# Mixer projections split at 400 and 240 tokens, first feed-forward loaded in three groups

## The chip, the cores and the metric

The kernel runs on one core of a Trainium2 chip. Its time is the device time of one launch in microseconds (us); three runs of the kernel before gave 3033.8, 3035.15 and 3030.21 us, median 3033.8. TensorE (PE in the rows) multiplies matrices, VectorE (DVE), ScalarE (ACT) and GpSimd (POOL) work on tiles, and SyncE (SP) issues the DMAs.

## The reference

One decoder layer over 1040 tokens (16 learned meta tokens and 1024 of the input), 1024 channels, in float32:

```
h = concat([meta, x])
h = h + 0.5 * swiglu(rms_norm(h, ffn1_norm), ffn1_w_in, ffn1_w_out)
h = h + hybrid_mixer(rms_norm(h, mix_norm), w_in, ...)     # DeltaNet branch | retention branch
h = h + 0.5 * swiglu(rms_norm(h, ffn2_norm), ffn2_w_in, ffn2_w_out)
out = rms_norm(h, final_norm)[:, 16:]
```

The mixer projects the normed tokens with one matrix of 1024 rows into queries, keys, values and gates of both branches (8 heads of 128 columns each), and two times 1024 columns for the merging gates. In the retention branch queries and keys are turned by a rotary table before the scan over chunks.

## The kernel before

Channels lie on the partitions and tokens along the free dimension. Each float32 operand is split into a high and a low part in the fp32r type, and `mm3` (L155 to L160) issues three matmuls for one product: high by high, high by low, low by high. A split (`split`, L135) is a copy on ScalarE and a subtraction on GpSimd, or on VectorE where the caller asks for it (`eng=V`).

The program runs through these stages: loading, transposing and norming the tokens for the first feed-forward (`start_group`, `start_operands`); the first feed-forward; `tail1`, which adds its last part and makes the mixer's operands; the retention heads (`ret_proj`, `ret_scan`); the gates and the DeltaNet heads, woven together; the output products; the second feed-forward.

A mixer projection takes a pair of output columns (128 each) at a time. Its scheme saves products: the tokens are cut into two halves of `HM` and a rest of `RM`, and the 1024 channels into two halves of four 128-row pieces. For the two token halves seven products (with sums of weights and sums of operands) replace eight; each is 4 pieces x 3 matmuls = 12 matmuls of HM columns, 84 a pair. The rest is computed plainly (`plain`): 16 pieces x 3 = 48 matmuls of RM columns a pair. With HM = 344, RM is 352. There are 40 such pairs: 16 for retention, 16 for DeltaNet, 8 for the gates. Beside them, the same token blocks (`MIX3`) cut the last part of the first feed-forward (48 matmuls a block) and the small products of `ab_products` (24, 24 and 36 split over the blocks: 60 of HM columns, 24 of RM).

For the first two retention heads the plain part and two of the products come ahead (`project_plain`, four pairs), since they need only the operands of the rest and of the first half; the operands of the five other products are made meanwhile on VectorE, ScalarE and GpSimd from the last block of the first feed-forward. Then `project_rest` does the five products; there `eng` is V, so its five weight splits a pair run on VectorE.

The order on each engine is not the order of the text: a scheduler places the instructions, and `tc.issue_after` keeps one behind another. Each engine works off its own list in order. `rotary` (L862) multiplies by a table on VectorE and GpSimd; L649 is the addition that brings a product out of PSUM.

Of the kernel before, what the change touches and what calls it, by code (L numbers as in the profile page):

```python
# [16 lines left out]
P = 128  # L17
# [29 lines left out]
    return [(a, b - a) for a, b in zip(edges, edges[1:])]  # L47


HM = 344  # L50
RM = T - 2 * HM
MIX3 = _cut([0, HM, 2 * HM, T])
REAL3 = _cut([NM, HM, 2 * HM, T])
# [43 lines left out]
def hybrid_layer(ctx, tc, a):  # L97
# [86 lines left out]
    def norm_stats(hT, b0, bn, sqs, last=None):  # L184
        for q in range(4):
            h = hT[:, 2 * q:2 * q + 2, b0:b0 + bn]
            if q == 3 and last:
                last.tensor_tensor(out=sqs[q], in0=h, in1=h, op=ALU.mult)
            else:
                S.activation(sqs[q], h, AF.Square)  # L190
        for q in range(1, 4):
            V.tensor_tensor(out=sqs[0], in0=sqs[0], in1=sqs[q], op=ALU.add)
        w = span_of(bn)
        ns = bn // w
        ps = psum("rx")
# [10 lines left out]
    def slots_of(ts, hn, n):  # L206
        return [[t[:, 4 * hn * i:4 * hn * i + 4 * hn].rearrange("p (k n) -> p k n", k=4) for t in ts] for i in range(n)]
# [67 lines left out]
    def ffn(fp, hidp, hT, hn, slots, spare, second, w_in, w_out, last_blocks, last_weights, tail, first, w0=None):  # L275
# [202 lines left out]
        for b0, bn in last_blocks:  # L478
# [5 lines left out]
                V.scalar_tensor_tensor(out=hs, in0=ps, scalar=0.5, in1=hs, op0=ALU.mult, op1=ALU.add)  # L484
            tail(b0, bn)


    f_ctx = ExitStack()
    fp = f_ctx.enter_context(tc.tile_pool(name="ffn1", bufs=4, side="right"))
# [46 lines left out]
        V.tensor_scalar(st1[:, 2, ts], st1[:, 2, ts], EPS, None, op0=ALU.add)  # L536
        rsqrt(st1[:, 3, ts], st1[:, 2, ts])

    def start_operands(grp):
        if grp == 0:  # L540
            halves = operand_halves(hidp, HN1)
            ts = [xp.tile([P, 16 * HN1], F32R, name="ox", tag="x" + t, bufs=1) for t in "HL"]
            slots[0].update(zip((0, 1, 4, 6), slots_of(ts, HN1, 4)))
        else:
            ts = [pool.tile([P, 3, 4, HN1], F32, name="b" + t, tag="e" + t, bufs=1) for pool, t in ((hidp, "H"), (fp, "L"))]
            halves = [ts[0][:, 0], ts[0][:, 1], ts[0][:, 2], ts[1][:, 0]]
            spare.extend(npool.tile([P, KC * T], F32R, name="on", tag=n) for n in ("nH", "nL"))
            slots[1].update(enumerate(slots_of(spare, HN1, 7)))
        for e in range(2):
            b0 = (2 * grp + e) * HN1  # L550
            pc = []
            for t in range(-1, NCH):
                c0, rows = (0, NM) if t < 0 else (NM + t * P, P)
                lo, hi = max(c0, b0), min(c0 + rows, b0 + HN1)
                if lo < hi:
                    pc.append((lo - b0, hi - lo, rows, lo - c0, st1[:, 3, t + 1:t + 2]))
            normed_half(hT, V_F1, b0, HN1, pc, *halves[2 * e:2 * e + 2])
        operand_blocks(slots[grp], halves, [E1[grp][i] and V or G for i in range(4)])
        return halves

    def start_differences():
# [6 lines left out]
        t = hidp.tile([P, 2, KC, P], F32R, name="ohl", tag="eH", bufs=1)  # L568
        return [[t[:, e, 4 * i:4 * i + 4] for e in range(2)] for i in range(2)]

    start_group(range(-1, 4))
    start_group(range(4, NCH))
    halves = [start_operands(grp) for grp in range(2)]
    h_d = tc.dram_tile([KC, P, SEQ], F32, name="h_d")
    ops, rest, kept, rows = [], [], [], []
    r_ctx = ExitStack()
# [1 line left out]
    def tail1(b0, bn):  # L578
        if not ops:
            n2 = [npool.tile([P, KC * T], F32R, name="act", tag=n) for n in ("nH", "nL")]  # L580
            x2 = [xp.tile([P, 16 * HN1], F32R, name="act", tag=n) for n in ("xH", "xL")]
            ops.extend(slots_of(n2, HM, 5) + slots_of(x2, HM, 2))
            for ts, o in ((n2, 20 * HM), (x2, 8 * HM)):
                rest.extend([t[:, o + k * RM:o + k * RM + RM] for t in ts] for k in range(4))
            kept.append(fp.tile([P, 12 * HN1], F32, name="sq", tag="eL", bufs=1))
        sq = kept[0][:, :KC * bn].rearrange("p (q k n) -> p q k n", q=4, k=2)
        ps = bcast(norm_stats(hT, b0, bn, [sq[:, q] for q in range(4)]), bn)

        def tmp():
            return fp.tile([P, 2 * HN1], F32, name="nrm", tag="tmp", bufs=5)[:, :bn]  # L590

        def put(i, k, src, eng):
            split(src, ops[i][0][:, k], ops[i][1][:, k], eng)

        def minus(out, x, y, eng):
            eng.tensor_tensor(out=out, in0=x, in1=y, op=ALU.subtract)

        if b0 == HM:
            hid_ctx.close()
            rows.append(r_ctx.enter_context(tc.tile_pool(name="rows", bufs=1, reuse_waits="tile")))  # L600
        if b0 == 2 * HM:
            for k in range(KC):
                n = tmp()
                normed(n.unsqueeze(1), hT, V_MIX, k, b0, bn, ps)
                split(n, *rest[k], V if k % 4 == 0 else G)
        elif b0 == 0:
            kept.append(ps)
            for k in range(KC):
                n = tmp()
                normed(n.unsqueeze(1), hT, V_MIX, k, b0, bn, ps)  # L610
                put(k // 4, k % 4, n, V if k % 4 == 0 else G)
        else:
            for k in range(4):
                b11, b21, b12, b22 = (kept[0][:, bn * i:bn * i + bn] if k % 2 else tmp() for i in range(4))
                for n, kk, t0, bc in ((b11, k, 0, kept[1]), (b12, k, HM, ps), (b22, k + 4, HM, ps), (b21, k + 4, 0, kept[1])):
                    normed(n.unsqueeze(1), hT, V_MIX, kk, t0, bn, bc)
                minus(b12, b12, b11, V)
                put(6, k, b22, V if k % 2 else G)
                minus(b22, b22, b12, V)
                put(2, k, b22, V)  # L620
                minus(b11, b22, b11, G)
                put(3, k, b11, G)
                put(4, k, b12, V)
                minus(b21, b21, b22, G)
                put(5, k, b21, G)
# [19 lines left out]

    H1, H2 = slice(0, HM), slice(HM, 2 * HM)

    def add(out, x, ps):
        V.tensor_tensor(out=out, in0=x, in1=ps, op=ALU.add)  # L649

    def product(w, i, ps=None, last=True, grow=False):
        first = ps is None
# [16 lines left out]
    def project_plain(raws, d0, d1, perm):  # L669
        a11, a12, a21, a22 = (put_weights(r, perm) for rs in raws for r in rs)  # L670
        yield from plain((a11, a12), d0)
        S.copy(d0[:, H2], (yield from product(a11, 0)))
        add(d0[:, H1], d0[:, H2], (yield from product(a12, 1)))
        yield from plain((a21, a22), d1)
        return a22

    def project_rest(raws, d0, d1, perm, a22=None):
        rg, ru = raws
        eng = None if a22 else V
        if a22 is None:  # L680
            a22 = put_weights(ru[1], perm, eng)
        V.tensor_tensor(out=ru[1], in0=ru[0], in1=ru[1], op=ALU.add)
        V.tensor_tensor(out=ru[0], in0=rg[0], in1=ru[0], op=ALU.subtract)
        V.tensor_tensor(out=rg[0], in0=ru[1], in1=rg[0], op=ALU.subtract)
        s2, s3 = put_weights(rg[0], perm, eng), put_weights(ru[0], perm, eng)
        V.tensor_tensor(out=rg[1], in0=rg[1], in1=rg[0], op=ALU.subtract)
        s1, s4 = put_weights(ru[1], perm, eng), put_weights(rg[1], perm, eng)
# [82 lines left out]
        return z[:, NM:]  # L770

    def cblk(n, pool):
        return pool.tile([P, 3 * P], F32, name="cb", tag="cb", bufs=2)[:, :n]

    ctab = tp.tile([P, T], F32, name="ctab")
    stab = tp.tile([P, T], F32, name="stab")
# [86 lines left out]
    def rotary(o):  # L863
        for b0, bn in MIX3:
            s = slice(b0, b0 + bn)
            sw = cblk(bn, rp)
            S.copy(sw[0:64], o[64:128, s])
            S.copy(sw[64:128], o[0:64, s])
            V.tensor_tensor(out=o[:, s], in0=o[:, s], in1=ctab[:, s], op=ALU.mult)
            G.tensor_tensor(out=sw, in0=sw, in1=stab[:, s], op=ALU.mult)  # L870
            V.tensor_tensor(out=o[:, s], in0=o[:, s], in1=sw, op=ALU.add)
        return o
# [689 lines left out]
```

## Time and profile before

| | |
|---|---|
| median of three runs | 3033.8 us |
| profiled execution, its own time | 3034.08 us |
| span from first to last instruction | 3032.3 us |
| TensorE busy | 2901.9 us (96%) |
| VectorE, ScalarE, GpSimd busy | 1824.1, 1341.1, 1644.4 us |
| mean granted TensorE clock | 0.978 of full |

A busy share says how much of the span an engine had an instruction in it; which engine sets the end is read stage by stage. TensorE's records overlap, since matmuls are pipelined: the pace is read from how many start in a stretch, not from the length of one. A row of windows gives the busy time of PE, PEld (weight load), DVE, ACT and POOL in that order, each with its count, then the clock, the share of the DMA engines and GB/s. "128x344" after an instruction is partitions by columns.

### The profile page before, as it was taken

The numbers are of one execution on the slowest core, as the hardware profiler recorded it, in microseconds if no ns is written. First come the engines' busy times: TensorE is split into PE (matmuls) and PEld (weight loads), VectorE is DVE, ScalarE is ACT, GpSimd is POOL, SyncE is SP. The second block draws the span as 40 slices with busy tenths as digits, with TensorE's granted clock in tenths as the row PEclk, the third lists the DMA queues.
The fourth block names the chain that finished last, engine by engine and source line by source line (L and its number), as shares of the span: only waits on it lengthen the run. The fifth ranks groups of instructions, "written<-read, shape, count | busy, mean of one in ns | idle before, by whom it ended". The sixth has DMA issues, their size and how long they took to land. (4 is left out here: it accounts for less than half of the span.)

```text
span 3032.3 us, 55807 instructions
## 1 busy us (share of the span) xinstructions
PE 2901.9 (96%) x21463; PEld 2751.1 (91%) x21463; DVE 1824.1 (60%) x3311; ACT 1341.1 (44%) x2801; POOL 1644.4 (54%) x1411
## 2 busy tenths in 40 slices
PE   7999999999999999988999999999999999998998
PEld 6999998999889999988999899988889999998877
DVE  8456557777775455455545555562338655557765
ACT  5333334433544655444555555563224433334432
POOL 5555556654655776543555554545426655557653
PEclk8999999999999999989999999999999999999999
DMA  3455557633311221212212222253533355457632
GB/s 104 137 172 160 166 172 255 211 93 119 85 50 43 67 69 58 73 46 63 76 53 64 64 82 63 58 181 113 179 102 111 117 172 170 161 162 252 209 115 94
DMA packets 368686, 359.23 MB, mean 118 GB/s; under 512 B 29073, under 2 KB 298642, under 8 KB 365858
## 3 DMA queue, kind: packets, MB, share of 16 engines
q1 hardware_dynamic: 368352, 355.64, 37.7%
q8 instruction: 168, 2.75, 0.4%
q14 instruction: 100, 0.82, 0.1%
q10 hardware_dynamic: 66, 0.02, 0.0%
HBM read 265.27 MB, written 90.32 MB: 117 GB/s over the span
## 5 line engine op out<-in xcount | busy, mean ns | idle before, releaser
L137 POOL TENSOR_TENSOR wl<-wraw,wh 128x512 fp32r<-128x512 f32 x798 | 1094.1, 1378 | 1008.3 <-ACT wh L136 940.0
L136 ACT CAST wh<-wraw 128x512 fp32r<-128x512 f32 x866 | 536.7, 623 | 976.2 <-issue 235.6
L1032 DVE SCALAR_TENSOR_TENSOR cb<-raw,cw,cb 128x344 f32<-128x344 f32 (+2 forms) x216 | 133.7, 652 | 25.1 <-ACT cb L1030 23.7
L223 DVE TENSOR_TENSOR wraw<-wraw 128x512 f32<-128x512 f32 x42 | 49.7, 1182 | 161.5 <-DMA wraw<-ffn_w_in 143.6
L158 PE MATMUL ps_gate_mm<-act,wh 128*128 128x344 f32 (+1 forms) x352 | 122.4, 348 | 6.0 <-DVE raw L649 3.9
L158 PE MATMUL ps_start_mm<-on,wh 128*128 128x260 f32 x392 | 111.6, 285 | 3.9 <-DVE q L295 2.3
L160 PE MATMUL ps_gate_mm<-act,wl 128*128 128x344 f32 (+1 forms) x352 | 114.2, 324 | 0.0
L159 PE MATMUL ps_gate_mm<-act,wh 128*128 128x344 f32 (+1 forms) x352 | 114.2, 324 | 0.0
L158 PE MATMUL ps_ffn_mm<-on,wh 128*128 128x256 f32 (+1 forms) x376 | 109.6, 292 | 2.0 <-ACT q L339 1.6
L159 PE MATMUL ps_start_mm<-on,wh 128*128 128x260 f32 x392 | 111.1, 283 | 0.0
L160 PE MATMUL ps_start_mm<-on,wl 128*128 128x260 f32 x392 | 110.8, 283 | 0.2 <-POOL wl L137 0.2
L160 PE MATMUL ps_ffn_mm<-on,wl 128*128 128x256 f32 (+1 forms) x376 | 109.5, 291 | 0.0
L159 PE MATMUL ps_ffn_mm<-on,wh 128*128 128x256 f32 (+1 forms) x376 | 109.2, 290 | 0.0
L158 PE MATMUL ps_start_px<-on,wh 128*128 128x260 f32 x308 | 87.5, 284 | 1.9 <-DVE sg L295 1.9
L298 DVE TENSOR_TENSOR q<-q,q 128x260 f32<-128x260 f32 (+1 forms) x84 | 69.7, 830 | 31.8 <-ACT q L339 31.8
L160 PE MATMUL ps_start_px<-on,wl 128*128 128x260 f32 x308 | 87.7, 285 | 0.0
L159 PE MATMUL ps_start_px<-on,wh 128*128 128x260 f32 x308 | 87.6, 285 | 0.0
L159 PE MATMUL ps_start_mm<-ox,wh 128*128 128x260 f32 x292 | 83.6, 286 | 3.6 <-DVE ox L137 3.6
L158 PE MATMUL ps_start_mm<-ox,wh 128*128 128x260 f32 x292 | 84.1, 289 | 1.7 <-ACT ox L136 1.2
L160 PE MATMUL ps_start_mm<-ox,wl 128*128 128x260 f32 x292 | 84.0, 288 | 0.6 <-POOL wl L137 0.6
L388 DVE TENSOR_TENSOR sums<-sums 128x512 f32<-128x512 f32 x80 | 83.8, 1068 | 0.7
L160 PE MATMUL ps_ffn_px<-on,wl 128*128 128x256 f32 (+1 forms) x284 | 83.2, 293 | 0.7 <-POOL wl L137 0.7
(1651 smaller groups left out, 10925.4 us busy)
## 6 DMA issues: line engine op xcount, KB each, us to landing
wraw<-ffn_w_in SPq DMA_DIRECT2D x176, 256.0 KB
wraw<-w_in SPq DMA_DIRECT2D x176, 256.0 KB
sums<-ffn_w_out SPq DMA_DIRECT2D x80, 256.0 KB
sums_d<-sums SPq DMA_DIRECT2D x20, 1024.0 KB
wraw<-sums_d SPq DMA_DIRECT2D x80, 256.0 KB
opnd<-opnd_d SPq DMA_DIRECT2D x35, 520.0 KB
opnd<-opnd_d SPq DMA_DIRECT2D x35, 512.0 KB
wraw<-ffn_w_out SPq DMA_DIRECT2D x68, 256.0 KB
```

Source lines behind the costliest of these rows:

```text
L136: S.copy(hi, raw)
L137: (eng or G).tensor_tensor(out=lo, in0=raw, in1=hi.bitcast(F32), op=ALU.subtract)
L158: PE.matmul(ps, lhsT=wh, rhs=xh, start=first and i == 0, stop=False, skip_group_check=grow)
L159: PE.matmul(ps, lhsT=wh, rhs=xl, start=False, stop=False, skip_group_check=grow)
L160: PE.matmul(ps, lhsT=wl, rhs=xh, start=False, stop=last and i == n - 1, skip_group_check=grow)
L223: V.tensor_tensor(out=ru[0], in0=ru[0], in1=ru[1], op=ALU.add)
L298: V.tensor_tensor(out=x[:, grp], in0=x[:, grp], in1=g[:, grp], op=ALU.mult)
L388: tc.keep_in_program_order(V.tensor_tensor(out=out, in0=x, in1=y, op=op))
L1032: conv[which] = V.scalar_tensor_tensor(out=c, in0=raw[:, s0 + k:s0 + k + n], scalar=cw[:, 24 * k + ct:24 * k + ct + 1], in1=c, op0=ALU.mul ...
```

## The change

`HM` becomes 400, so `RM` is 240. The operands no longer fit where they lay: the sums of squares get three slots in place of four, the last operand lies in four pieces in two places (`Pieces`), and the scratch tile `cb` grows. `project_rest` loses its `eng`, so its splits go to GpSimd. `rotary`'s first multiplication is placed behind the last `add` of the projection. `norm_stats` adds each square as soon as it is there. The tokens of the first feed-forward are loaded and normed in three groups: the tiles that the first quarter of the tokens needs, those of the second quarter, and the rest.

```diff
-HM = 344
+HM = 400
 RM = T - 2 * HM
...
-        for q in range(1, 4):
-            V.tensor_tensor(out=sqs[0], in0=sqs[0], in1=sqs[q], op=ALU.add)
+            if q:
+                V.tensor_tensor(out=sqs[0], in0=sqs[0], in1=sqs[q], op=ALU.add)
...
-    def start_operands(grp):
+    def start_operands(grp, tiles):
...
         for e in range(2):
+            if tiles[e]:
+                start_group(tiles[e])
             b0 = (2 * grp + e) * HN1
...
-    start_group(range(-1, 4))
-    start_group(range(4, NCH))
-    halves = [start_operands(grp) for grp in range(2)]
+    halves = [start_operands(0, (range(-1, 2), range(2, 4))), start_operands(1, (range(4, NCH), ()))]
...
-        sq = kept[0][:, :KC * bn].rearrange("p (q k n) -> p q k n", q=4, k=2)
-        ps = bcast(norm_stats(hT, b0, bn, [sq[:, q] for q in range(4)]), bn)
+        sq = kept[0][:, :6 * bn].rearrange("p (q k n) -> p q k n", q=3, k=2)
+        ps = bcast(norm_stats(hT, b0, bn, [sq[:, q] for q in (0, 1, 2, 1)]), bn)
...
     def add(out, x, ps):
-        V.tensor_tensor(out=out, in0=x, in1=ps, op=ALU.add)
+        added[0] = V.tensor_tensor(out=out, in0=x, in1=ps, op=ALU.add).ins
...
-    def project_rest(raws, d0, d1, perm, a22=None):
+    def project_rest(raws, d0, d1, perm):
         rg, ru = raws
-        eng = None if a22 else V
-        if a22 is None:
-            a22 = put_weights(ru[1], perm, eng)
+        a22 = put_weights(ru[1], perm)
...
-        s2, s3 = put_weights(rg[0], perm, eng), put_weights(ru[0], perm, eng)
+        s2, s3 = put_weights(rg[0], perm), put_weights(ru[0], perm)
...
-            V.tensor_tensor(out=o[:, s], in0=o[:, s], in1=ctab[:, s], op=ALU.mult)
+            with tc.issue_after(added[0]):
+                V.tensor_tensor(out=o[:, s], in0=o[:, s], in1=ctab[:, s], op=ALU.mult)
```

VectorE's list at the start of the program, before: `st` holds the statistics, `small` the diagonal that spreads them, `lower` and `ox` the first operands.

```order
L532 SCALAR_TENSOR_TENSOR st_102<-xnL 128x1
L519 BN_STATS xnL<-xnH 128x6 x2
L172 TENSOR_SCALAR small<-ident,st_102 16x16
L172 TENSOR_SCALAR small<-ident,st_102 128x128
L172 TENSOR_SCALAR small<-ident,st_102 128x116
L172 TENSOR_SCALAR small<-ident,st_102 128x12
L172 TENSOR_SCALAR small<-ident,st_102 128x128
L172 TENSOR_SCALAR small<-ident,st_102 128x120
L172 TENSOR_SCALAR small<-ident,st_102 128x8
L529 COPY hT<-ps_start_mm 128x4x128
L531 BN_AGGR xnL<-xnL 128x2
L181 SCALAR_TENSOR_TENSOR lower<-hT,wv,ps_start_px 128x260 x4
```

The same place now (the numbers of lines moved by some, L526 is L519 of before, L536 is L529, L539 is L532).

```order
L172 TENSOR_SCALAR small<-ident,st_102 16x16
L172 TENSOR_SCALAR small<-ident,st_102 128x128
L172 TENSOR_SCALAR small<-ident,st_102 128x116
L172 TENSOR_SCALAR small<-ident,st_102 128x12
L538 BN_AGGR xnL<-xnL 128x2
L536 COPY hT<-ps_start_mm 128x4x128
L539 SCALAR_TENSOR_TENSOR st_102<-xnL 128x1
L536 COPY hT<-ps_start_gx 128x4x128
L526 BN_STATS xnL<-xnH 128x6 x2
L542 TENSOR_TENSOR st_102<-st_102 128x2
L181 SCALAR_TENSOR_TENSOR lower<-hT,wv,ps_start_px 128x260 x4
L181 SCALAR_TENSOR_TENSOR upper<-hT,wv,ps_start_px 128x260 x4
```

The diagonal of the first quarter of the tokens now stands ahead of the statistics of tile 5, and the normed operands ahead of those of tile 7.

VectorE's list where `project_rest` of head 0 begins, before: `wl` is the low part of a split weight, `wraw` a sum of weights, `rkq` a query or key row.

```order
L686 TENSOR_TENSOR wraw<-wraw 128x512
L137 TENSOR_TENSOR wl<-wraw,wh 128x512 x4
L649 TENSOR_TENSOR rkq<-rkq,ps_r0proj_mm 128x344
L137 TENSOR_TENSOR wl<-wraw,wh 128x512
L682 TENSOR_TENSOR wraw<-wraw 128x512
L649 TENSOR_TENSOR rkq<-rkq,ps_r0proj_mm 128x344
L683 TENSOR_TENSOR wraw<-wraw 128x512
L684 TENSOR_TENSOR wraw<-wraw 128x512
L649 TENSOR_TENSOR rkq<-rkq,ps_r0proj_mm 128x344 x2
L686 TENSOR_TENSOR wraw<-wraw 128x512
L137 TENSOR_TENSOR wl<-wraw,wh 128x512 x2
L649 TENSOR_TENSOR rkq<-rkq,ps_r0proj_mm 128x344
```

And now (L663 is L649 of before, L693 to L697 are L682 to L686).

```order
L697 TENSOR_TENSOR wraw<-wraw 128x512
L663 TENSOR_TENSOR rkq<-rkq,ps_r0proj_mm 128x400 x2
L693 TENSOR_TENSOR wraw<-wraw 128x512
L694 TENSOR_TENSOR wraw<-wraw 128x512
L663 TENSOR_TENSOR rkq<-rkq,ps_r0proj_mm 128x400 x2
L695 TENSOR_TENSOR wraw<-wraw 128x512
L697 TENSOR_TENSOR wraw<-wraw 128x512
L663 TENSOR_TENSOR rkq<-rkq,ps_r0proj_mm 128x400
L663 TENSOR_TENSOR rv<-rv,ps_r0proj_mm 128x400
```

The splits are gone from VectorE's list. On GpSimd they stand behind the last operands (`act`) of the mixer; there the list reads now:

```order
L137 TENSOR_TENSOR act<-sq,act 128x400
L882 TENSOR_TENSOR cb<-cb,stab 128x400
L137 TENSOR_TENSOR act<-nrm,act 128x400 x2
L137 TENSOR_TENSOR wl<-wraw,wh 128x512
L137 TENSOR_TENSOR act<-sq,act 128x400
L137 TENSOR_TENSOR wl<-wraw,wh 128x512 x8
L702 TENSOR_TENSOR rkq<-rkq 128x400
L137 TENSOR_TENSOR wl<-wraw,wh 128x512 x3
```

Before, three splits and the addition of L691 (now L702) stood behind the last `act` there, and a run of rotary products behind them.

## Rows read from the trace of the kernel before

**Rows 1.** Windows by stage: stretch, length, busy and count of each engine, clock, DMA.

```profile
0.00:31.00 31.00, 15.55 (x89) 13.20 (x89) 24.13 (x56) 19.72 (x43) 11.31 (x16) 0.83 0.71 228
31.00:81.00 50.00, 41.22 (x275) 38.97 (x276) 48.76 (x61) 20.95 (x40) 34.31 (x23) 0.84 0.07 22
81.00:737.00 656.00, 645.90 (x5271) 642.95 (x5272) 421.79 (x721) 249.24 (x508) 359.69 (x261) 0.99 0.51 164
737.00:809.00 72.00, 63.66 (x378) 60.53 (x377) 54.99 (x88) 34.94 (x73) 55.50 (x48) 0.93 0.41 126
809.00:870.00 61.00, 54.01 (x318) 49.78 (x317) 53.35 (x90) 31.70 (x59) 25.35 (x24) 0.94 0.28 74
870.00:1230.00 360.00, 350.68 (x2301) 334.21 (x2300) 199.35 (x419) 192.08 (x359) 236.24 (x233) 1.00 0.20 57
1230.00:2028.00 798.00, 758.37 (x6498) 725.30 (x6498) 441.33 (x1050) 419.42 (x973) 386.35 (x402) 0.97 0.24 69
2028.00:3032.30 1004.30, 972.53 (x6344) 886.18 (x6342) 580.39 (x831) 373.02 (x751) 535.62 (x408) 0.98 0.48 154
```

**Rows 2.** Windows of unbroken fp32r matmuls of 260, 256, 512, 344 and 352 columns.

```profile
100.00:200.00 100.00, 100.00 (x835) 99.91 (x834) 56.80 (x85) 37.45 (x84) 52.87 (x40) 1.00 0.48 154
2500.00:2600.00 100.00, 100.00 (x843) 100.00 (x842) 56.80 (x86) 38.26 (x86) 55.84 (x42) 1.00 0.48 156
2100.00:2200.00 100.00, 100.00 (x433) 80.61 (x432) 35.59 (x36) 29.19 (x45) 54.23 (x37) 1.00 0.57 176
809.00:820.30 11.30, 11.30 (x73) 11.11 (x72) 8.31 (x14) 6.03 (x10) 1.24 (x1) 1.00 0.36 93
763.40:767.10 3.70, 3.70 (x26) 3.70 (x24) 3.70 (x8) 2.21 (x4) 2.95 (x3) 1.00 0.36 88
```

**Rows 3.** Timeline of TensorE: start, length, instruction, count; matmuls of one column between.

```profile
1314.42 0.32 PE L159 MATMUL ps_g1proj_mm<-act,wh 128*128 128x344 f32 x1
1314.58 0.83 PE L1080 MATMUL ps_g0q_gx<-ones,cb 128*128 128x1 f32 x6
1315.27 0.40 PE L160 MATMUL ps_g1proj_mm<-act,wl 128*128 128x344 f32 x1
```

**Rows 4.** Groups of TensorE: count, busy us, mean ns; plain fp32 matmuls.

```profile
L992 PE MATMUL ps_decay_px<-em,masks 128*128 128x512 f32 x32 | 15.7, 592 | 0.0
```

**Rows 5.** Timeline of VectorE at the start.

```profile
17.30 5.55 DVE L172 TENSOR_SCALAR small<-ident,st 16x16 f32<-16x16 f32 x7
23.48 1.61 DVE L181 SCALAR_TENSOR_TENSOR lower<-hT,wv,ps_start_px 128x260 f32<-128x260 f32 x4
29.90 2.76 DVE L137 TENSOR_TENSOR ox<-lower,ox 128x520 fp32r<-128x520 f32 x2
```

**Rows 6.** Timeline of all engines at the start: GpSimd's first splits, TensorE's first wait.

```profile
17.44 4.99 POOL L137 TENSOR_TENSOR wl<-wraw,wh 128x512 fp32r<-128x512 f32 x4 [1.37 <-ACT wh L136]
...
31.01 0.59 PE L159 MATMUL ps_start_mm<-ox,wh 128*128 128x260 f32 x1 [3.63 <-DVE ox L137]
```

**Rows 7.** Groups of GpSimd from 764 to 801 us.

```profile
L137 POOL TENSOR_TENSOR wl<-wraw,wh 128x512 fp32r<-128x512 f32 x11 | 17.5, 1599 | 2.4 <-ACT wh L136 2.4
L137 POOL TENSOR_TENSOR act<-nrm,act 128x344 fp32r<-128x344 f32 x6 | 6.0, 1019 | 0.0
L596 POOL TENSOR_TENSOR nrm<-nrm 128x344 f32<-128x344 f32 x4 | 4.7, 1200 | 0.0
L596 POOL TENSOR_TENSOR sq<-sq 128x344 f32<-128x344 f32 x4 | 4.3, 1087 | 0.0
L137 POOL TENSOR_TENSOR act<-sq,act 128x344 fp32r<-128x344 f32 x4 | 3.9, 993 | 0.0
```

**Rows 8.** Groups of VectorE from 809 to 870 us.

```profile
L137 DVE TENSOR_TENSOR wl<-wraw,wh 128x512 fp32r<-128x512 f32 x17 | 11.4, 683 | 6.5 <-ACT wh L136 6.4
```

**Rows 9.** Groups of GpSimd from 801 to 870 us.

```profile
L137 POOL TENSOR_TENSOR wl<-wraw,wh 128x512 fp32r<-128x512 f32 x5 | 7.3, 1468 | 0.0
```

**Rows 10.** Waits of TensorE from 1230 to 2028 us: waiting, waited for, us, times.

```profile
PE ps_g5scan_gx L1310 <- DVE st L1320: 4.5, 1, 4.5
```

More of the change, by code (lines that the diff above doesn't have):

```diff
@@ L485, in ffn, with __init__, __getitem__ @@
             tail(b0, bn)
+    class Pieces:
+        def __init__(self, parts):
+            self.parts = parts
+        def __getitem__(self, key):
+            return self.parts[key[1]]
     f_ctx = ExitStack()
@@ L557, in start_operands @@
             normed_half(hT, V_F1, b0, HN1, pc, *halves[2 * e:2 * e + 2])
-        operand_blocks(slots[grp], halves, [E1[grp][i] and V or G for i in range(4)])
+            for i in (2 * e, 2 * e + 1):
+                put_slot(slots[grp][(0, 1, 4, 6)[i]], halves[i], E1[grp][i] and V or G)
         return halves
@@ L581, in tail1 @@
             x2 = [xp.tile([P, 16 * HN1], F32R, name="act", tag=n) for n in ("xH", "xL")]
-            ops.extend(slots_of(n2, HM, 5) + slots_of(x2, HM, 2))
-            for ts, o in ((n2, 20 * HM), (x2, 8 * HM)):
-                rest.extend([t[:, o + k * RM:o + k * RM + RM] for t in ts] for k in range(4))
+            ops.extend(slots_of(n2, HM, 5) + slots_of(x2, HM, 1))
+            rest.extend([t[:, 4 * HM + k * RM:4 * HM + k * RM + RM] for t in x2] for k in range(KC))
+            last = [t[:, 4 * HM + KC * RM:5 * HM + KC * RM] for t in x2]
             kept.append(fp.tile([P, 12 * HN1], F32, name="sq", tag="eL", bufs=1))
-        sq = kept[0][:, :KC * bn].rearrange("p (q k n) -> p q k n", q=4, k=2)
-        ps = bcast(norm_stats(hT, b0, bn, [sq[:, q] for q in range(4)]), bn)
+            kept.append(last)
+        sq = kept[0][:, :6 * bn].rearrange("p (q k n) -> p q k n", q=3, k=2)
+        ps = bcast(norm_stats(hT, b0, bn, [sq[:, q] for q in (0, 1, 2, 1)]), bn)
         def tmp():
@@ L599, in tail1 @@
             hid_ctx.close()
+            op = x_ctx.enter_context(tc.tile_pool(name="op", bufs=1))
+            o2 = [op.tile([P, 3, HM], F32R, name="act", tag=n) for n in ("oH", "oL")]
+            ops.append([Pieces([first, *(t[:, k] for k in range(3))]) for first, t in zip(kept.pop(1), o2)])
             rows.append(r_ctx.enter_context(tc.tile_pool(name="rows", bufs=1, reuse_waits="tile")))
@@ L646, in hybrid_layer @@
     H1, H2 = slice(0, HM), slice(HM, 2 * HM)
+    added = [None]
     def add(out, x, ps):
-        V.tensor_tensor(out=out, in0=x, in1=ps, op=ALU.add)
+        added[0] = V.tensor_tensor(out=out, in0=x, in1=ps, op=ALU.add).ins
     def product(w, i, ps=None, last=True, grow=False):
@@ L674, in project_plain @@
         yield from plain((a21, a22), d1)
-        return a22
-    def project_rest(raws, d0, d1, perm, a22=None):
+    def project_rest(raws, d0, d1, perm):
         rg, ru = raws
-        eng = None if a22 else V
-        if a22 is None:
-            a22 = put_weights(ru[1], perm, eng)
+        a22 = put_weights(ru[1], perm)
         V.tensor_tensor(out=ru[1], in0=ru[0], in1=ru[1], op=ALU.add)
@@ L684, in project_rest @@
         V.tensor_tensor(out=rg[0], in0=ru[1], in1=rg[0], op=ALU.subtract)
-        s2, s3 = put_weights(rg[0], perm, eng), put_weights(ru[0], perm, eng)
+        s2, s3 = put_weights(rg[0], perm), put_weights(ru[0], perm)
         V.tensor_tensor(out=rg[1], in0=rg[1], in1=rg[0], op=ALU.subtract)
-        s1, s4 = put_weights(ru[1], perm, eng), put_weights(rg[1], perm, eng)
+        s1, s4 = put_weights(ru[1], perm), put_weights(rg[1], perm)
         S.copy(d1[:, H1], (yield from product(a22, 5)))
@@ L772, in cblk @@
     def cblk(n, pool):
-        return pool.tile([P, 3 * P], F32, name="cb", tag="cb", bufs=2)[:, :n]
+        return pool.tile([P, 4 * P], F32, name="cb", tag="cb", bufs=2)[:, :n]
     ctab = tp.tile([P, T], F32, name="ctab")
```

## The prediction

> **What bounds the kernel now.** I read the windows by stage first: TensorE is busy in 96% of the span, and what it is idle is spread: about 15.5 us before 31 us, 8.8 in 31 to 81, 8.3 in 737 to 809, 7.0 in 809 to 870, 39.6 in 1230 to 2028, and about 3% or less of each other stage [rows 1]. So the time is TensorE's pace times the number of columns, plus short stretches where another engine is full. The reader is to see two of these in the same rows: in 31 to 81 VectorE is busy 48.76 us of 50, and in 737 to 809 GpSimd 55.5 of 72; its groups from 764 to 801 add up to 17.5 + 6.0 + 4.7 + 4.3 + 3.9 = 36.4 us of 37 [rows 7]. In 809 to 870 VectorE is busy 53.35 of 61. Next I read the pace from windows in which nothing interrupts TensorE [rows 2]: 100 us hold 835 matmuls of 260 columns (119.8 ns each), 843 of 256 (118.6) and 433 of 512 (230.9). A line through 260 and 512 has (230.9 - 119.8)/252 = 0.441 ns a column. It gives 156.8 ns at 344, and the row there has 11.3 us/72 = 156.9; at 352 it gives 160.4, and the short window (3.7 us, 26 with those cut at its edges) allows 154 to 161. Last, the start: TensorE's unbroken work begins at 31.01 us, after a wait of 3.63 us for VectorE's split [rows 6].
>
> **Columns.** 40 pairs x 84, 96 of the first feed-forward's tail and 60 small ones make 3516 matmuls of HM columns; 40 x 48 + 48 + 24 = 1992 are of RM. The line gives 181.5 ns at 400, 24.7 more than at 344: 3516 x 24.7 = +86.8 us. For 240 columns no row exists, and this decides the sign. From below: the line, 111.0 ns, so 1992 x 49.4 = -98.4 and the sum is -11.6 us. From above, among fp32r rows: no faster than 256 columns, 118.6 ns, so -83.3, sum +3.5. Between them lies the nearest row to a limit: six matmuls of one column with their 128x128 weights start within 1315.27 - 1314.58 = 0.69 us, 115 ns each, though they have next to no columns to stream [rows 3]; that is the pace of loading weights. 115 would give -90.4, sum -3.6. I take 113, halfway between the line and that row, whose last start falls after a switch to another form: 1992 x 47.4 = -94.4, **sum -7.6 us**. The gain is lost at 116.8 ns. Much farther out lies plain fp32: 16 matmuls of 512 columns make 32 records with 856 ns a matmul at 428 from record to record by the timeline; the group's row shows the records 592 ns long [rows 4], overlapped. Were 240 columns to run so, each would take some 400 ns.
>
> **Start.** The seven diagonals take 5.55 us on VectorE from 17.30, while GpSimd runs four splits from 17.44 to 22.43; `lower` comes at 23.48, the split of `ox` at 29.90 [rows 5, 6]. In the new list three of the seven diagonals and the statistics of two tiles no longer stand ahead of `lower`, so the first matmul should come some 7 us earlier, at about 24. But VectorE is full until 81 us, and the same work is only told off in another order: what can be gained is VectorE's idle time before 31 us, 31.0 - 24.13 = 6.9 us, and part of that is the wait for the tokens (DMA share 0.71). I take a little over half: **-4** (0 to -7).
>
> **Mixer operands, 737 to 809.** Here GpSimd's list decides. Its operand work of 6.0 + 4.7 + 4.3 + 3.9 = 18.9 us grows by 400/344, +3.1 us. And the plain parts of four pairs, which run meanwhile, get 192 x 47.4 = 9.1 us shorter while two products a pair (96 matmuls) get 2.4 longer: 6.7 us that the column sum counts as won, but that TensorE can't have while it waits for GpSimd. Together 9.8. GpSimd is full in 37 of the 72 us, and TensorE has other work in the rest: I take two thirds, **+7** (0 to +10). The squares in three slots add one wait, of the last square for the second sum; VectorE has 17 us free there, and I count 0.
>
> **First two heads, 809 to 870.** 20 splits leave VectorE: 17 in this stage, 683 ns each with 6.4 us of waits for ScalarE's copy in front of them [rows 8], 13.7 us in all. TensorE is idle 7.0 us here, and VectorE is what it waits for. On GpSimd a split takes 1.468 us [rows 9]: 20 x 1.468 = 29.4, with its 25.35 busy us that is 54.8 of 61, and a pair's five splits (7.3 us) lie beside 60 x 181.5 = 10.9 us of products. So it keeps pace, with little to spare. Behind the splits in GpSimd's list stand head 0's rotary products (L882); the retention scan waits for those, and it is covered by the projection of the next head. I take **-5** (-7 to +8; the upper end is half of what 20 splits are longer, 20 x 0.785 = 15.7, uncovered).
>
> **Small edits.** The rotary pin puts a multiplication behind the last addition of its head; the additions, which free PSUM for TensorE, come earlier, and the scan's queries later. TensorE is idle 9.3 us in 870 to 1230, over six heads 1.6 a head. Taken 0 (-2 to +3). Evictions of 400 columns are longer by a sixth and those of 240 shorter by a third; no engine beside TensorE is over two thirds busy after 870 us, which hides that.
>
> **Sum.** -7.6 - 4 + 7 - 5 = -9.6 us. The profiled execution took 3034.1 us, 1.8 more than its span of 3032.3; it is the median (3033.8) within 0.3. So **3024 us**.
>
> **Rivals.**
> **A, weights set a floor.** If loading 128 columns of weights takes longer than streaming 240 columns, a narrower matmul gains nothing: 118.6 ns as at 256, columns +3.5, total +3.5 - 4 + 7 - 5 = +1.5, 3035.5 us. For it: 256 and 260 differ by 1.2 ns where the line has 1.8, and 115 ns with no columns. Against it: 115 is still below 118.6.
> On this the Trainium skill has a rule, in "TensorE: Matmul & The Clock Gate", section "LDWEIGHTS (loading the stationary operand)": a load of P columns takes about P/1.2 ns, 106.7 at 128, and section "Back-to-back issue gap" has N/2.4 + 2.5 ns for an isolated matmul. As an estimate from these pages 240 columns would be held at 106.7 rather than 102.5, and the column sum would be 1992 x 42.5 against 3516 x 23.3, -2.7 us, the total about 3029. The rule speaks against going below 256; the trace agrees that there is a floor, and puts it higher, at 115.
> **B, GpSimd binds the first heads.** No relief and +8 in place of -5: -7.6 - 4 + 7 + 8 = +3.4, 3037.5 us. For it: 54.8 of 61 us, after a stage that ends with GpSimd behind. Against it: 7.3 us of splits to 10.9 of products.
> **C, slower.** In 1230 to 2028 the DeltaNet chains run beside projections. 24 pairs there lose 24 x 48 x 47.4 ns = 54.6 us of plain work, and their products grow by 24 x 84 x 24.7 = 49.8. If the chains are what sets the pace where plain parts cover them, the 54.6 don't come in full: a third missing is +18, 3042 us; from 10 us (18%) on nothing is left of my gain. For it: 39.6 us idle, and single waits such as 4.5 us for `st` [rows 10]. Against it: that is 5% of the stage, and the scheduler can fill the longer products instead.
> **D, better.** GpSimd's lateness before 809 costs nothing (0 for +7) and the start gives 7: -7.6 - 7 - 5 = -19.6, 3014 us. For it: TensorE has 8.3 us idle there already, which may take up the shift.
> **E, narrow fp32r drops to plain fp32's pace.** 1992 x (401 - 113) = +574, about 3600 us. For it: no fp32r matmul before is narrower than 256. Against it: 256 and 260 show nothing that begins.
>
> **How the numbers follow.** Forecast 0.46 (its own range 3017 to 3031), A 0.15, B 0.12, C 0.10, D 0.14, E 0.03. A change under 0.2%, 6 us, can't be told from none, as the three runs lie 5 us apart. Faster than 3027.7: three quarters of the forecast's share (0.35), D, and 0.05 of A and B: 0.54. Slower than 3039.9: most of C, E, and a third of B: 0.15. Same: 0.31. The range of 8 in 10 goes from 3012, past D, to 3041, past B; E stays outside.
>
> **What would show it.** The starts of 240-column matmuls in an unbroken stretch: 111 to 115 ns for me, 118 for A, 400 for E; of 400 columns 181 to 182. The first unbroken matmul near 24 us, and VectorE's full stretch ending by some 4 us before 81. GpSimd's full stretch before the first heads some 3 us longer, TensorE's idle time up by up to 7 there, and down to about 2 in the first two heads; if that stage has waits for `wl` from GpSimd, B holds. Idle time in 1230 to 2028 staying near 39.6; above 50 is C. I am wrong if 240 columns take over 116.8 ns, or if the idle time grows outside 737 to 809.

## The result and the profile after

The changed kernel takes 3071.03 us (median of four, 3069.44 to 3074.95) against 3032.01 us before (3028.7 to 3035.15): a ratio of 1.0133, interval 1.0115 to 1.0152. It is slower by some 39 us, where I had forecast 10 us faster and given a range to 3041. The profiled execution took 3069.44 us, its span is 3067.7, 35.4 more than before.

The windows by stage, with edges at the same places of the program as in [rows 1] and the same columns (length; busy time and count of PE, PEld, DVE, ACT, POOL; granted clock; DMA share; GB/s):

```profile
0.00:31.00 31.00, 20.84 (x123) 19.07 (x124) 23.03 (x60) 17.73 (x40) 11.21 (x16) 0.89 0.71 228
31.00:81.00 50.00, 39.31 (x259) 36.85 (x258) 48.33 (x60) 23.62 (x46) 36.97 (x24) 0.86 0.11 33
81.00:729.50 648.50, 637.70 (x5236) 635.07 (x5237) 425.14 (x719) 247.04 (x505) 362.04 (x261) 0.99 0.51 165
729.50:801.00 71.50, 59.68 (x371) 56.33 (x370) 51.69 (x81) 35.80 (x68) 56.27 (x48) 0.88 0.40 127
801.00:861.00 60.00, 56.09 (x326) 54.24 (x325) 40.55 (x64) 27.09 (x52) 45.52 (x39) 0.97 0.28 70
861.00:1232.00 371.00, 353.19 (x2285) 332.56 (x2284) 215.94 (x424) 196.84 (x361) 236.66 (x235) 1.00 0.20 56
1232.00:2067.00 835.00, 776.54 (x6521) 735.39 (x6520) 456.65 (x1059) 421.30 (x981) 392.69 (x405) 0.95 0.23 66
2067.00:3067.70 1000.70, 968.25 (x6343) 881.76 (x6341) 582.30 (x831) 373.13 (x751) 534.92 (x408) 0.99 0.48 154
```

Up to 861 us the changed kernel is ahead: the three stages that I had worked out one by one end 9 us earlier than before. The stage of the retention heads (360 us before) takes 371, and the one after it 835 for 798: there TensorE's idle time went from 39.6 to 835.00 - 776.54 = 58.5 us and its clock from 0.97 to 0.95. These 48 us, less the 9 us ahead and 3.6 won behind 2067, are the 35 us of the result.

Most of them lie in one place. From the first gate matmul to the first DeltaNet projection, before and (second fence) after; and from the second DeltaNet head's projection to the third's, the same way:

```profile
1229.70:1255.40 25.70, 25.70 (x178) 25.66 (x177) 11.34 (x27) 9.90 (x18) 12.62 (x14) 1.00 0.17 43
...
1305.90:1423.40 117.50, 103.22 (x853) 96.17 (x851) 66.12 (x166) 53.21 (x119) 43.03 (x42) 0.88 0.22 58
```

```profile
1233.00:1286.80 53.80, 38.72 (x219) 34.98 (x218) 21.21 (x53) 14.14 (x28) 19.07 (x28) 0.81 0.13 40
...
1336.90:1459.90 123.00, 108.53 (x851) 100.55 (x848) 66.16 (x167) 52.33 (x120) 42.99 (x42) 0.83 0.23 56
```

The first stretch doubles, by 28 us: TensorE is idle 15 us where it was never idle, and its clock reads 0.81 in place of 1.00, so what it does run, it runs slowly. The waits of TensorE and of ScalarE there (waiting, waited for, us, times, longest), and the instruction that TensorE's gate products stand behind:

```profile
PE ps_r7scan_px L977 <- DVE rog L976: 8.9, 2, 5.6
PE ps_gate_mm L158 <- ACT raw L681: 3.3, 1, 3.3
```

```profile
1267.87 0.36 ACT L681 COPY raw<-ps_gate_mm 128x240 f32<-128x240 f32 x1 [8.94 <-DMA yB_d<-rz]
```

ScalarE's copy of the first gate sum into its row `raw` waits 8.94 us for the DMA that stores the last z row (`rz`, the gate values of a retention head) of head 7. A row of one stage waits for a row of another, though neither computes from the other: they share memory. The addresses stand in the built programs, not in the trace. Before, the three `raw` rows began at byte 211360 of a partition and the z rows ended at 202944. With the tile pool `op` for the last operand and the larger `cb` the left side of memory grew until the second z row lies at 209408 to 213568, and the first `raw` row at 210336 to 214508. TensorE's list, as built, shows it as well: before, the matmuls of head 7's scan stand between gate and DeltaNet products, never more than nine together; now 45 matmuls of the scan stand in one block, and 96 gate matmuls wait behind it. The scan is a chain with waits for VectorE in it, and nothing fills them.

### The profile page after: what moved, and what is told of

It is laid out like the page before. It is cut to its first block, busy times and chain, and to the rows that moved or that the text cites. A ratio compares the mean times of both kernels' runs of the same rounds, so it can differ in the third digit from the quotient of the medians.

```text
span 3067.7 us, 55806 instructions
## 1 busy us (share of the span) xinstructions
PE 2911.6 (95%) x21451; PEld 2751.3 (90%) x21451; DVE 1843.6 (60%) x3291; ACT 1342.5 (44%) x2803; POOL 1676.3 (55%) x1432
## 5 line engine op out<-in xcount | busy, mean ns | idle before, releaser
L137 POOL TENSOR_TENSOR wl<-wraw,wh 128x512 fp32r<-128x512 f32 x818 | 1117.8, 1374 | 1042.8 <-ACT wh L136 989.5
L1044 DVE SCALAR_TENSOR_TENSOR cb<-raw,cw,cb 128x400 f32<-128x400 f32 (+2 forms) x216 | 137.2, 669 | 23.1 <-ACT cb L1042 21.7
L158 PE MATMUL ps_gate_mm<-act,wh 128*128 128x400 f32 (+1 forms) x352 | 124.5, 354 | 11.3 <-DVE raw L663 5.0
L159 PE MATMUL ps_gate_mm<-act,wh 128*128 128x400 f32 (+1 forms) x352 | 116.2, 330 | 0.0
L160 PE MATMUL ps_gate_mm<-act,wl 128*128 128x400 f32 (+1 forms) x352 | 115.9, 330 | 0.0
L158 PE MATMUL ps_ffn_px<-on,wh 128*128 128x256 f32 (+1 forms) x284 | 82.9, 292 | 1.0 <-ACT wh L136 1.0
```

The source lines that it names most:

```text
L137: (eng or G).tensor_tensor(out=lo, in0=raw, in1=hi.bitcast(F32), op=ALU.subtract)
L158: PE.matmul(ps, lhsT=wh, rhs=xh, start=first and i == 0, stop=False, skip_group_check=grow)
L159: PE.matmul(ps, lhsT=wh, rhs=xl, start=False, stop=False, skip_group_check=grow)
L160: PE.matmul(ps, lhsT=wl, rhs=xh, start=False, stop=last and i == n - 1, skip_group_check=grow)
L1044: conv[which] = V.scalar_tensor_tensor(out=c, in0=raw[:, s0 + k:s0 + k + n], scalar=cw[:, 24 * k + ct:24 * k + ct + 1], in1=c, op0=ALU.mul ...
```

## The experiments

Two theories at first. M: the shared memory costs the 28 us at the gates. P: the rotary pin (`issue_after` in `rotary`), which puts each scan behind its whole projection, costs them, and the 11 us of the retention heads too. Ratios are to the kernel before, run beside each, with their 95% intervals; between runs that do not stand together, differences of ratios are safer than those of times.

**e1_zlow**, the z rows' pool moved below the others, so that the gates' rows lie over a rotary table:

```diff
-    rp, tp, zp = (... for n in ("ret", "rot", "rz"))
+    zp, rp, tp = (... for n in ("rz", "ret", "rot"))
```

> The changed kernel with the pools of the retention rows entered in another order: the z rows (rz) lie lowest, the rotary tables on top, so that the gates' raw rows lie over a table and no longer over a z row. Pin kept. Theory M (memory: the gates' products are held back until the last z row is stored) expects the block of head 7's scan between 1232 and 1265 us to mix with gate products again, TensorE idle 1230 to 1290 back from 15 to under 6 us, and 25 to 33 us off the time: about 3041 us (3036 to 3047). Theory P (the rotary pin, which puts each scan behind its whole projection, is the cause) expects no change, 3066 to 3073.

3047.81 us, 1.0061 (1.0048 to 1.0075): 23 us less than the changed kernel (22 by the ratios), just under the 25 expected. The stretch from the gates to the first DeltaNet projection, after this edit:

```profile
1235.60:1264.20 28.60, 28.37 (x192) 27.05 (x191) 17.39 (x35) 13.29 (x27) 15.47 (x17) 1.00 0.18 47
```

28.6 us in place of 53.8, with 0.2 us idle at full clock. M holds.

**e2_nopin**, the changed kernel with the pin taken out:

```diff
-            with tc.issue_after(added[0]):
-                V.tensor_tensor(out=o[:, s], in0=o[:, s], in1=ctab[:, s], op=ALU.mult)
+            V.tensor_tensor(out=o[:, s], in0=o[:, s], in1=ctab[:, s], op=ALU.mult)
```

> The changed kernel without the rotary pin, memory as it was. Theory P expects head 7's scan to start some 20 us earlier, under its projection, the loss of 29 us at the first gates to go, and the 11 us between the third head and the gates with it: about 3032 us. Theory M expects the order to keep the gates behind the scan's end all the same; the scan begins earlier, so part of the 29 goes, 8 to 15 us, and the rest stays: 3055 to 3063.

3062.15 us, 1.0109 (1.0093 to 1.0125): 9 us less (7 by the ratios, whose intervals just meet). The stretch at the gates still takes 51.1 us, although head 7's scan starts 21 us earlier. P falls as the cause of it.

**e3_zlow_nopin**, both edits:

> Both edits: z rows lowest, and no rotary pin. If M and P each hold a part (M the 29 us at the gates, P the 11 us over heads 2 to 7), this is the only one of the four to come back to the kernel before or under it: 3024 to 3034. If the 11 us come from the wider products themselves, it ends near the version with the pin: 3036 to 3046.

3039.13 us, 1.0036 (1.0024 to 1.0049). The time lies in the second forecast, the one for losses that come from the wider products. By stage it is mixed: heads 2 to 7 take 365.7 us in place of 377.3 in e1, near the 362.7 of before, but the first two heads take 135.6 in place of 130.2.

**e4_pad**, the kernel before with an unused tile that pushes its z rows up under the gates' rows:

```diff
     stab = tp.tile([P, T], F32, name="stab")
+    tp.tile([P, 2912], F32, name="pad")
```

> The kernel before, with nothing changed but an unused tile of 11648 bytes a partition among the rotary tables, which pushes the z rows up until the gates' raw rows lie over one, as in the changed kernel. M expects 20 to 30 us more than before, lost between 1230 and 1290 us with the scan of head 7 in one block: 3052 to 3062. P, or any theory in which the sizes of the products or the start matter, expects the time of before, 3028 to 3036.

3055.76 us, 1.0095 (1.0078 to 1.0112), 26 us more than before (29 by the ratio) for a tile that nothing reads or writes. The same stretch in it:

```profile
1236.20:1287.70 51.50, 36.78 (x207) 34.48 (x206) 14.96 (x43) 11.28 (x20) 15.60 (x24) 0.80 0.14 41
```

15 us idle and a clock of 0.80, as in the changed kernel. The overlay is shown from both sides: taken away it gives 23 us, added it costs 26.

What was left: e3 is 9 us above before, though the start is faster. The next four take single parts.

**f1_start3**, the kernel before with the three token groups alone (the hunks of `start_operands` and its two calls from the diff above):

> The kernel before with one part of the change alone: tokens of the first feed-forward in three groups. My step (the start gains 4 us, 0 to 7) expects 3 to 8 us under the kernel before, about 3024 us, with the end of the first feed-forward's stage earlier by as much. The rival, that VectorE is full until 81 us in any order, expects the time of before within 2 us.

3022.36 us, 0.997 (0.9959 to 0.9981): 9 us faster, a little more than the 3 to 8 expected. The second head's projection begins 8.2 us earlier and what follows keeps at least that.

**f2_e3_restV**, e3 with `put_weights(..., perm, V)` in `project_rest`:

> As the version with z rows lowest and no rotary pin (9 us over the kernel before), but the splits of the first two heads' five remaining products stay on VectorE. If GpSimd is what makes TensorE wait 11.7 us in the second head's projection (5.3 before), this gains 4 to 8 us: 2 to 6 us over the kernel before. If the move to GpSimd helps, as my step said, it loses 3 to 7 us: 12 to 16 over.

3040.21 us, 1.0034 (1.0018 to 1.0049). By the whole time there is no difference to e3, which neither forecast had; by stage the first two heads take 129.1 us in place of 135.6, and some of it is lost further on.

**f3_e3_pin01**, e3 with the pin for heads 0 and 1 (`if h < 2:` ahead of it):

> As the version with z rows lowest and no pin, but with the rotary pin for heads 0 and 1 alone. The pinned versions reached the third head's projection 8 to 9 us before the kernel before did, the unpinned with z rows lowest only 0.6 us; they then lost 11 to 12 us by the gates. If the pin helps in the first two heads and hurts later, this keeps the first and avoids the second: 6 us better, 2 to 5 us over the kernel before. If those 6 us come from elsewhere: 8 to 10 over.

3047.65 us, 1.0049 (1.0029 to 1.0068). A miss: the first two heads are 5.8 us shorter than in e3 as expected, but the stage behind them is 7.8 us longer, though heads 2 to 7 have no pin here. TensorE waits in that stage for the scans of heads 0 and 1, which the pin moved into it (2.5 us for head 0's `rkt`), and 2.8 us in head 2's scan, a wait that f2 has without any pin.

**f4_e3_hm384**, e3 with another cut:

```diff
-HM = 400
+HM = 384
```

> As the version with z rows lowest and no pin, but the token cut at 384 and 272 in place of 400 and 240. By the paces in the trace (400 columns 183 ns, 240 columns 113 ns; 384 some 176, 272 some 125) the exchange is a wash: 84 x 7 ns against 48 x 12 ns a pair, so within 3 us of it, 7 to 12 us over the kernel before. Were the number of columns alone to count (192 more a pair at 0.457 ns), it would be 3.5 us worse. Were 240 columns to cost more elsewhere, in waits that their shorter plain parts no longer cover, it would be 4 to 8 us better.

3047.47 us, 1.0052 (1.0032 to 1.0073), 8 us over e3 by the medians and 5 by the ratios, which is not clear of their intervals. The paces are as forecast (174 and 126 ns), yet in the profiled execution each of the heads 5 to 7 takes 3 to 7 us longer than in e3, at a clock of 0.94 with waits of up to 1.4 us for `rog` in each scan. Neither column counts nor paces explain that; that it is where the scan's waits fall is not shown.

A third theory came from the trace of e3. There TensorE waits 6.7 us at once for an addition of VectorE; in the changed kernel the same wait is 5.5. VectorE's short operations of the first DeltaNet head's recurrence in the changed kernel (start, length), and GpSimd's at the same time:

```profile
1357.04 0.22 DVE L1182 TENSOR_TENSOR pr<-xr,u 128x72 f32<-128x72 f32 x1
...
1357.72 0.22 DVE L1183 TENSOR_TENSOR u<-u,pr 128x72 f32<-128x72 f32 x1
...
1361.81 0.97 DVE L1182 TENSOR_TENSOR pr<-xr,u 128x45 f32<-128x45 f32 x1
1362.81 0.96 DVE L1183 TENSOR_TENSOR u<-u,pr 128x45 f32<-128x45 f32 x1
1363.81 0.96 DVE L1182 TENSOR_TENSOR pr<-xr,u 128x36 f32<-128x36 f32 x1
...
1367.90 0.56 DVE L663 TENSOR_TENSOR raw<-raw,ps_g1proj_mm 128x400 f32<-128x400 f32 x1
```

```profile
1355.95 1.95 POOL L133 TENSOR_TENSOR rq<-rq,mhalf 128x8 f32<-128x8 f32 x1 [3.60 <-DVE rq L1098]
...
1361.66 1.05 POOL L1286 TENSOR_TENSOR kte<-kt,eg 128x512 f32<-128x512 f32 x1
1362.66 1.04 POOL L1287 TENSOR_TENSOR vt<-vt,v_s 128x512 f32<-128x512 f32 x1
1363.67 1.05 POOL L1286 TENSOR_TENSOR kte<-kt,eg 128x512 f32<-128x512 f32 x1
```

An operation of 45 columns takes 0.97 us where one of 72 took 0.22, and ends as GpSimd's current operation ends: one VectorE operation gets through per GpSimd operation. Not every GpSimd operation does this: the first of 72 columns took 0.22 us inside the 1.95 us of L133 on 8 columns. The addition (L663), for which TensorE waits, stands behind the slow ones. In e3 nine are slow in this recurrence: six beside GpSimd's products, three beside its weight splits (L137). The expectation below counts ten and puts all down to the products.

**h1_e3_coll**, e3 with these GpSimd products of head 0 on ScalarE:

```diff
+            if h == 0:
+                for i in range(4):
+                    S.activation(kte[gi][:, i], kt[gi][:, i], AF.Copy, scale=eg[:, c1 + i, h:h + 1])
+                    S.activation(vt[gi][:, i], vt[gi][:, i], AF.Copy, scale=v_s[:, c1 + i:c1 + i + 1])
+                    S.activation(kt[gi][:, i], kt[gi][:, i], AF.Copy, scale=kd_s[:, c1 + i:c1 + i + 1])
+                continue
```

> As the version with z rows lowest and no pin (9 to 11 us over the kernel before), but for the first DeltaNet head the six GpSimd products of its scan (keys and values times their decays) run on ScalarE, as 24 smaller ones. In the trace of that version ten short VectorE additions and multiplications of two operands (0.2 us each elsewhere) take 0.96 to 1.2 us while those GpSimd products run, and TensorE waits 6.7 us for the addition queued behind them. If that collision is the cause, the wait falls under 2 us and the time by 4 to 8 us; if VectorE is late for another reason, both stay.

3030.82 us, 1.0006 (0.9994 to 1.0018): 8 us less than e3 (9 by the ratios). Two short operations are still slow there, both beside weight splits. TensorE's wait for the addition, in e3 and in this one:

```profile
PE ps_g1proj_mm L158 <- DVE raw L663: 10.6, 2, 6.7
```

```profile
PE ps_g1proj_mm L158 <- DVE raw L663: 3.8, 2, 2.6
```

The longest wait is 2.6 us, not quite under the 2 expected. The stretch of this head went from 116.9 to 103.4 us, its clock from 0.88 to 0.98: more than the wait itself comes back.

**h3_f1_coll**, the same edit on f1:

> The three groups alone on the kernel before (9 us under it), with the same six GpSimd products of the first DeltaNet head on ScalarE. There the chain of short VectorE operations is nearly over when the GpSimd products begin, so little should come of it: 0 to 4 us further under the kernel before. A gain as large as in the other version would mean that the collision is not what sets that one apart.

3014.89 us, 0.9952 (0.9936 to 0.9967): 7 us less than f1 (5 by the ratios, whose intervals just meet), where I expected 0 to 4. What gave it is not shown. In f1, as in the kernel before, six of the short operations are slow, but only one of them runs beside a product that was moved; five run beside weight splits, and five such are still slow here. What went is a wait of 2.8 us for the scan's state `st` and most of one for `Tc` (2.0 to 0.4). So the gain is no difference of the cut, and the collision is worse at 400 by a few operations. This version beats both kernels, by 15 and 56 us.

**p1_before_pin**, the kernel before with the pin alone:

> The kernel before with the rotary pin alone. In the runs so far the stretch from the third head's projection to the gates took 374 to 377 us with the pin and 366 to 368 without it (362.7 in the kernel before). If the pin makes this by itself, the stretch takes 370 to 374 us here, and head 7's scan ends later beside the gates, which are free here: 8 to 14 us over the kernel before. If the 400-column products are needed for it, as by my step that costed the pin at nothing, the time is that of before within 3 us.

3028.62 us, 0.9996 (0.9986 to 1.0005): no change. **p2_start3_restP**, f1 with `project_rest`'s splits on GpSimd:

> The kernel before with the three groups and with the splits of the first two heads' five remaining products on GpSimd, no pin and the old token cut. The three groups alone were 9 us under the kernel before. If the move to GpSimd frees VectorE as my step said, this is 12 to 16 us under; if the rotary products that stand behind the splits in GpSimd's list make the first two heads wait, as the unpinned versions with 400 columns show (135 us from the first head to the third, 129 with the splits on VectorE), it is 1 to 5 us under.

3029.4 us, 0.9999 (0.9986 to 1.0012): 7 us more than f1, 9 by the ratios. At 344 the move to GpSimd costs; it does not help. The loss is not in the first two heads, which get 2.5 us shorter (129.1 to 126.6), but behind them: 7.0 us in heads 2 to 7 and 4.6 in the second DeltaNet head.

Last, two kernels alike in all but the cut and the memory plan that goes with it: **q1_400_all** is the changed kernel with z rows lowest, splits on VectorE and the six products on ScalarE; **q2_344_all** is the kernel before with the three groups, the pin, and the same products on ScalarE.

> The changed kernel with the three losses found so far taken out and the pin kept: z rows lowest, the splits of the first two heads' remaining products on VectorE, and the first DeltaNet head's six products on ScalarE. From the first head to the gates the version with neither pin nor GpSimd splits took 496.6 us (492.4 in the kernel before). If the pin gives 11 us there as it did at the old cut, this takes 486 and the whole 3016 to 3024 us; if the pin gives nothing at 400, it takes 495 to 500 and the whole 3028 to 3036.

> The same set at the old token cut of 344 and 352: the kernel before with the three groups, the rotary pin, splits on VectorE, and the six products on ScalarE. The three groups and the products alone were 15 us under the kernel before; with the pin 1 to 6 more: 3009 to 3014 us. Against the version at 400 this shows what the cut itself is worth with all else alike: by the paces in the trace 400 should be 4 to 5 us faster; if its waits eat that, it is level or slower.

3031.68 us, 1.0012 (0.9999 to 1.0025), and 3019.59 us, 0.9956 (0.9942 to 0.9971). So q2 misses its 3009 to 3014. With all else alike the cut of 400 is 12 us slower (17 by the ratios). Two pairs above differ in no more than these either, both without the pin: f2 against f1 by 18 us (19 by the ratios), e3 against p2 by 10 (11). The loss is idle time: TensorE is busy 2898.8 of q1's 3035.1 us and 2899.9 of q2's 3023.2, idle 136.3 and 123.3. The stretch from the third retention head to the gates, at 344 and (second fence) at 400:

```profile
848.10:1211.50 363.40, 354.16 (x2309) 336.12 (x2307) 191.96 (x421) 182.82 (x352) 235.00 (x233) 1.00 0.20 57
```

```profile
852.50:1228.60 376.10, 358.73 (x2317) 337.68 (x2316) 220.07 (x427) 198.57 (x364) 239.97 (x239) 0.99 0.19 56
```

TensorE's idle time in it is 9.2 us at 344 and 17.4 at 400, and VectorE is busy 28 us longer. The stages of all these, in us, cut where TensorE starts each (heads r0, r1 / heads r2 to r7 / gates / first DeltaNet projection / second):

| kernel | cut, pin, splits on | r0, r1 | r2 to r7 | gates | g0 | g1 | ratio |
|---|---|---|---|---|---|---|---|
| before | 344, no, VectorE | 129.7 | 362.7 | 25.6 | 50.6 | 117.4 | 1 |
| p1 | 344, yes, VectorE | 117.0 | 364.1 | 29.4 | 54.8 | 117.1 | 0.9996 |
| f1 | 344, no, VectorE | 129.1 | 362.7 | 25.6 | 50.6 | 115.4 | 0.997 |
| p2 | 344, no, GpSimd | 126.6 | 369.7 | 25.6 | 50.6 | 120.0 | 0.9999 |
| q2 | 344, yes, VectorE | 116.8 | 363.4 | 29.4 | 53.5 | 117.4 | 0.9956 |
| changed | 400, yes, GpSimd | 128.4 | 374.9 | 53.8 | 50.1 | 123.0 | 1.0133 |
| e1 | 400, yes, GpSimd | 130.2 | 377.3 | 28.6 | 54.5 | 118.0 | 1.0061 |
| e3 | 400, no, GpSimd | 135.6 | 365.7 | 26.1 | 56.0 | 116.9 | 1.0036 |
| f2 | 400, no, VectorE | 129.1 | 367.5 | 26.1 | 55.9 | 118.4 | 1.0034 |
| q1 | 400, yes, VectorE | 121.8 | 376.1 | 28.6 | 55.9 | 107.3 | 1.0012 |

Read down a column: at 344 the pin shortens the first two heads by 13 us and leaves the next six alone; at 400 it shortens the first two by 5 to 7 and lengthens the next six by 9 to 12. Part of that is a shift: the pin moves scan work of heads 0 and 1 behind the edge between the two columns (f3). In q2's g1 the moved products bring nothing against p1, although TensorE's idle time there falls from 14.3 to 10.6 us: the granted clock is 0.85 for 0.88. Five short operations still run slowly beside GpSimd's weight splits, as many as in h3, whose stretch takes 105.4; why q2's does not is open.

## Why the prediction was wrong

**The step that failed is "small edits", taken at 0 (-2 to +3).** I costed the pin and the longer evictions there and gave no term at all to where the wider operands lie. The overlay of a z row by the gates' rows costs 23 to 26 us (e1, e4; 22 to 29 by the ratios). The pin's 0 held at 344 (p1); at 400 it costs 9 us (7 to 8 by the ratios: the changed kernel against e2, e1 against e3). The list of TensorE's instructions showed the overlay ahead of the run, and the forecast rested on the lists of VectorE and GpSimd at two other places. A second step failed beside it, "columns": its paces were right, its sum was not.

**Columns, -7.6.** The paces are as forecast. Two unbroken stretches of the changed kernel, 400 and 240 columns (the first matmul of each and the one behind the last):

```profile
1215.01 0.34 PE L160 MATMUL ps_r7proj_mm<-act,wl 128*128 128x400 f32 x1
...
1217.20 0.34 PE L160 MATMUL ps_r7proj_mm<-act,wl 128*128 128x400 f32 x1
...
1217.93 0.27 PE L158 MATMUL ps_r7proj_mm<-act,wh 128*128 128x240 f32 x1
...
1220.62 0.35 PE L158 MATMUL ps_r7proj_mm<-act,wh 128*128 128x400 f32 x1
```

12 of 400 in 2.19 us are 182.5 ns (181.5 forecast), 24 of 240 in 2.69 us are 112.1 ns (113 forecast, 116.8 the point where nothing is left). 3516 x 25.7 - 1992 x 48.3 = -5.9 us. So rivals A and E fall: no floor at 118.6, no plain fp32 pace. The 115 of [rows 3] is no floor for these matmuls either, as the prediction had it under A: 112.1 lies below it. (Those six records are three matmuls in plain fp32, two records each.) But the sum of paces isn't what the cut is worth. Three pairs say that it costs 10 to 19 us; q1 against q2 it costs 12, 18 worse than its paces, in waits. Of the 13 us of idle time that q1 has more, 8 lie in heads 2 to 7.

**Start, -4.** The mechanism was right and the term too small: TensorE's unbroken work begins at 24.00 us as forecast,

```profile
24.00 0.58 PE L159 MATMUL ps_start_mm<-ox,wh 128*128 128x260 f32 x1 [0.63 <-DVE ox L137]
```

seven us before that of [rows 6], and f1 gives 9 us, beyond the edge of my range at -7. VectorE was busy 24.13 + 48.76 = 72.9 us of the first 81 before and 23.03 + 48.33 = 71.4 after, so I was right that it is full there, and wrong that this keeps the gain under its idle time: TensorE, with 5.3 us less idle time before 31 us, came out ahead.

**Mixer operands, +7.** The stage got 0.5 us shorter. GpSimd's operand work there grew by 1.9 us (5.8 + 5.1 + 5.0 + 4.9 for 18.9, where I had 3.1), and TensorE's idle time rose from 8.3 to 11.8, half of the 7; TensorE was busy 4.0 us less, so part of the 6.7 us that I had counted as lost came in. By name it waits there for ScalarE's part of the operand splits (2.7 us before, 4.0 after) more than for GpSimd's `wl` (0.4 and 1.0).

**First two heads, -5.** Idle time fell from 7.0 to 3.9 us, and the stage shortened by 1. But alone the move to GpSimd costs 7 to 9 us (p2). That is about rival B's price, but B's mechanism is not shown. Its sign, waits for `wl` from GpSimd in that stage, is absent in the changed kernel, and in p2 the loss lies behind the stage. Without the pin at 400 the first two heads do take longer with the splits on GpSimd, 135.6 us for 129.1 (e3, f2), and the whole time stays the same. The wait that f1 and f2 lack there is one of TensorE for ScalarE's gate values `rz` of head 1, in e3 and in p2:

```profile
PE ps_r1proj_mm L158 <- ACT rz L780: 3.9, 1, 3.9
...
PE ps_r1proj_mm L158 <- ACT rz L770: 4.2, 1, 4.2
```

**Rival D**'s two terms both came: the start gave 9 us and the mixer operands cost nothing. The rest buried them.

**Rival C** had the place, 1230 to 2028 us, and the sign, and by my own mark (idle time above 50) it would hold. Its mechanism does not: from the third DeltaNet projection on, the rest of that stage takes 606.9 us for 604.8. The loss is at the entry of it. By the prediction's last sign, idle time that grows outside 737 to 809, it was wrong.

**The account.** f1 -9; the move to GpSimd +7 to +9; the overlay +23 to +26; the cut by itself +12 to +17; the pin about 0. Together +33 to +43, where +39 was measured. That is a check of size and no proof: the terms come from different kernels, and two of them change with the others. The move to GpSimd makes no difference at 400 without the pin (e3, f2), and the pin costs 9 us at 400, which the term of the cut holds in part, since q1 and q2 both have it. What stays open is why the cut adds idle time, and why with the pin heads 2 to 7 take 9 to 12 us longer at 400 and no longer at 344. In the changed kernel TensorE's waits in heads 4 to 6 are for the rotated queries and the scan's first state, some 2 us a head; no run separated that from the places in which the scheduler put the scans.

## What to carry to other kernels

A change of tile sizes moves memory, and memory that two stages share can be a wait: look at what lies over what, and in the bound engine's list whether the next stage's work still stands between the last stage's chain. A sum of matmul paces is not yet what a finer cut brings: here it said -6 us and the cut cost 10 to 19, in idle time between products. Test an edit apart from its companions: here one part alone was 9 us faster and was buried by the others.

## What the hardware showed

An unused tile cost 26 us through addresses alone (e4). A short operation of VectorE with two operands from SBUF took as long as the product or weight split that GpSimd was running: 0.96 to 1.2 us in place of 0.2. The Trainium skill has the rule, in "SBUF — State Buffer", section "Who interferes with whom": a VectorE instruction with two inputs from SBUF contends with a GpSimd instruction that reads SBUF. The trace agrees for the products, with one operation of 0.96 to 0.97 us let through per GpSimd operation of 1.04 to 1.05, but not for GpSimd's 1.95 us on 8 columns (L133), inside which one kept its 0.22 (the profile's spans of GpSimd are rough). Lost time also comes double where TensorE's clock follows: the stretch at the gates was idle for 15 us and lost 28, with the granted clock at 0.81, between its levels of 1.2 and 2.4 GHz (0.5 and 1.0).
